# Third quarters of the weights loaded at the first copy, another set of six pairs and a planner that counts SyncE's queue, in a two-layer encoder kernel

## The chip, the cores and the metric

The kernel runs on one core of a Trainium2 chip. The metric is the device time of one execution, in microseconds (us). Three runs of the kernel before have a median of 2688.19 us (2686.57 to 2691.58).

## The reference, cut to what matters

A trunk of two layers works on x, 256 tokens by 4096 channels, in float32. Each layer multiplies the normalised x by one large matrix `w_in` (4096 x 11264), does attention with 16 heads (4 for keys and values) on a part of the result and a bidirectional retention with 8 heads on another, gates both, and multiplies the 4096 channels of the outcome by `w_out` (4096 x 4096). The result is added to x, and a last norm follows.

```python
for l in range(DEPTH):                      # 2 layers
    h = rmsnorm(x, norm_w[l])
    proj = h @ w_in[l]                      # 256 x 4096 by 4096 x 11264
    aq, ak, av, ag, rq, rk, rv, rg = jnp.split(proj, SPLIT_POINTS, axis=-1)
    aq = axial_rope(rmsnorm(aq)) * attn_scale
    ak = axial_rope(rmsnorm(ak))
    a_out = silu(ag) * gqa_attention(aq, ak, av)          # softmax(q k^T) v
    rq, rk = axial_rope(rq), axial_rope(rk) * ret_scale
    r = bidirectional_retention(rq, rk, rv, log_gf, log_gb)
    r_out = silu(rg) * rmsnorm(r, ret_norm[l])
    x = x + jnp.concatenate([a_out, r_out], axis=-1) @ w_out[l]
return rmsnorm(x, final_norm)
```

## The kernel before, in words

**The products.** The columns of the two weight matrices are cut into blocks of 1024 (two times 512): 11 blocks of `w_in` and 4 of `w_out` in each layer, 30 in all. A block runs over 16 pairs of row tiles (a pair is 256 rows of weights), and adds up in eight banks, `M1` to `M8`. A float32 weight is not multiplied as it is: ScalarE casts it to a rounded high half (`whi`), VectorE subtracts that from the weight to make the low half (`wlo`), and each product is three matmuls, high by high (weights `whi`, operand `x8h` or `x7h`), high by low (`x8l` or `x7l`) at L1605, and low by high at L1615.

**Eights and sevens.** Ten of the 16 pairs of a block, the eights, have eight products and two pages of weights; a page is 128 x 1024 numbers (512 KB) and is loaded by SyncE into the tile `wraw` (L490; six places). The other six pairs, the sevens (the table `SEVENS`, L91), use a scheme with seven products in place of eight. They need sums of the weights' quarters: page A is the first load (`wraw`; two quarters), page T the tile `wv`, made by ScalarE as a copy of A (L643), to which GpSimd (POOL) adds the second quarter by an accumulating DMA (L645, issued by `add` at L663). The *third quarter* is loaded by SyncE into the tile `third` (256 KB, L507; two places). Page U (`wu`) is A plus `wv` plus `third`, two additions on VectorE (L601 and L602). Page B is the third quarter itself, of which `bhi` (ScalarE) and `blo` (VectorE) are the halves, one place each (L553). There are 30 x 6 = 180 third quarters.

**The order.** Every engine takes its instructions in the order in which the program is written, and this order is set by a planner in the program itself. It keeps an estimated time `now.t` for TensorE, and for VectorE (`ve`) and ScalarE (`ac`) an estimated time until which they are busy (`Clock`, L273). Constants stand for what loads take: `RAW_LANDING` (6.0 us) for a `wraw` or `third`, `ADD_LANDING` (11.0 us) from the end of the copy `wv` to the accumulated sum.
- `load` (L484) issues the next `wraw` as soon as the low half of an old one is written (`empty`). 
- `begin` (L582) makes the halves of a page. With page A of a seven it raises `wanted` and calls `load_third` (L501), which issues the load of the third quarter if one of the two places is free; a place counts as free when the matmuls on page B are done (`release`, L517, which raises `done`). With page T it writes the two additions of `wu` and has VectorE's estimate wait for `wv` and `third` (L600).
- `halve` (L620) makes the halves of page B once the page before has been released and `wu` has been written.
- `add_up` (L630) makes the copy `wv` when A has landed by the estimate, up to two ahead (`SUMS`).
- `low_parts` writes the low halves that are due; `parts` (L550) keeps them in the list `later`, with a function `then` that is called behind the low half.

**The other work.** Attention, retention, norms and stores run as tasks between the products of a block: `tick` (L1001) runs a step when `room` finds time for it. `startable` (L952) names the next task to begin: if the pages of a task don't suffice, a later one may go ahead, except past a task that needs `STRICT` or more pages. `AT_ONCE` (L83) says up to how many tasks `running` (L967) counts when it lets another begin. The sequences of such a task: the attention scores `attention_pair` (L1165) take one free bank of `M1`, `M5`, `M6`, `M7` between two blocks (`take_bank`, L886), multiply into it (L1081 to L1083), VectorE takes the maximum (`st`), ScalarE the exponentials (`pr`), and the bank is free again. `attention_values` (L1210) fetches the turned exponentials (`pT`, L1048), splits them and multiplies them with the values. `combine` frees `M1` at the end of a block by a copy to `ca`. `retention_head` (L1336) takes a bank only if `LONG` more products than usual are left until it is needed.

**The opening.** In the first block of each of the four stages (two layers, `w_in` and `w_out`) the six sevens stand at the places that the tables `SPREAD` to `SPREAD3` name, since the operand x still arrives in chunks.

Most operations of VectorE and ScalarE are recorded at L289, in the helper that keeps the estimates, so they are told apart by their tiles.

Of the kernel before, what the change touches and what calls it, by code (L numbers as in the profile page):

```python
# [39 lines left out]
THIRDS = 2  # L40

RING = 5

STRICT = 9
RELIEF = 2.0
ADDED = 99
AHEAD = 6
# [16 lines left out]
MARGIN = 0.0  # L64

RAW_LANDING = 6.0
ADD_LANDING = 11.0
ADD_SLACK = 0.3

RUSH = 1.0  # L70
# [9 lines left out]
TIGHT_A = 2  # L80
TIGHT_B = 9

AT_ONCE = 3  # L83

WARM = 20

# [1 line left out]

START = 1

SEVENS = ((3, 5, 7, 9, 11, 13), (3, 5, 7, 9, 11, 13), (3, 5, 7, 9, 11, 13), (3, 5, 7, 9, 11, 13))  # L91

EVER = sorted(set(_p for _s in SEVENS for _p in _s))
EIGHTS = [_p for _p in range(NP) if _p not in EVER]
# [11 lines left out]

QUEUE = 1.0
LOW_AHEAD = 3.0
LONG = 2

NEAR = 30

# [68 lines left out]
GROUPS = [  # L181
    ([tuple(range(_s[0]))] if _s[0] else []) + [tuple(range(_a, _b)) for _a, _b in zip(_s, _s[1:] + (NP,))] for _s in SEVENS
]
SPREAD = (3, 6, 9, 10, 12, 14)
SPREAD1 = (4, 6, 8, 9, 11, 13)
SPREAD2 = (2, 4, 6, 7, 10, 12)
SPREAD3 = (5, 7, 8, 11, 12, 14)


# [114 lines left out]
def hybrid_encoder(  # L304
# [141 lines left out]
    class Weights:  # L446


        def __init__(self):
            self.pages, self.sevens = [], []  # L450
            for l in range(DEPTH):
                for w, n in ((w_in, N_IN), (w_out, N_OUT2)):
                    for b in range(n):
                        stage = 2 * l + (w is w_out)
                        start = (l, b) == (0, 0) and w is w_in
                        for g in GROUPS[stage] if b else FIRST_GROUPS[stage]:
                            for slot in slots_of(g, stage, start):
                                one = Page()
                                one.pair, one.kind, one.uses, one.left = slot[0][1], slot[0][3], len(slot), 3 * len(slot)
                                one.whole = start and one.pair in NATIVE  # L460
                                one.seven = one.pair in SEVENS[stage] and not one.whole
                                one.begun, one.low_at, one.empty = False, None, False
                                one.kept, one.half, one.own = None, one.seven and one.kind == PAGE_B, None
                                if w is w_out and (l, b) == (DEPTH - 1, n - 1) and one.pair in DELAYED:
                                    one.kept = 0 if one.kind == PAGE_A else 1
                                    one.uses, one.left = one.uses - 1, one.left - 3
                                if one.seven:
                                    if one.kind == PAGE_A:
                                        self.sevens.append(Seven(w[l, b, one.pair]))
                                    one.own = self.sevens[-1]  # L470
                                if not one.seven or one.kind == PAGE_A:
                                    one.src = w[l, b, one.pair, int(one.kind == PAGE_B)]
                                self.pages.append(one)
            self.wholes = [g for g in self.pages if g.whole]
            self.thirds = [g for g in self.pages if g.half]
            self.seq = [g for g in self.pages if not g.whole and not g.half]
            self.raws = [g for g in self.seq if not g.seven or g.kind == PAGE_A]
            self.placed, self.emptied, self.made = 0, 0, 0
            self.credit, self.at, self.granted, self.summed = 0, 0, 0, 0
            self.loaded, self.halved, self.done, self.wanted = 0, 0, 0, 0  # L480
            self.lows, self.spent = 0, 0
            self.later, self.adds = [], []

        def load(self):  # L484

            if self.placed < len(self.raws):
                g = self.raws[self.placed]
                self.placed += 1
                g.raw = t(wp, [P, 2, NB], "wraw", RAWS)
                nc.sync.dma_start(g.raw, g.src)  # L490
                if g.seven:
                    g.own.a, g.own.a_at = g.raw, max(now.t, ve.until) + RAW_LANDING

        def empty(self, g):

# [4 lines left out]

        def load_third(self):  # L501

            while self.loaded < min(self.wanted, self.done + THIRDS):
                o = self.thirds[self.loaded].own
                self.loaded += 1
                o.b = t(wp, [P, NB], "third", THIRDS)
                nc.sync.dma_start(o.b, o.third)  # L507
                o.b_at = now.t + RAW_LANDING

        def grant(self):  # L510

# [5 lines left out]
        def release(self, g):  # L517

            if g.half:
                self.done += 1  # L520
                self.load_third()
                self.halve()
                return
            self.credit += 1
# [57 lines left out]
        def begin(self, g):  # L582

            g.begun = True
            if not g.seven:
                self.parts(g, g.raw, then=partial(self.empty, g))
                return
            o = g.own
            if g.kind == PAGE_A:
                self.wanted += 1  # L590
                self.load_third()
                ac.after(o.a_at)
                self.parts(g, o.a)
# [14 lines left out]
            else:  # L608
                ac.after(o.u_at)
                self.parts(g, o.u)  # L610

        def spend(self):
            self.spent += 1

# [5 lines left out]
        def halve(self):  # L620

            if self.halved == self.done < len(self.thirds):
                g = self.thirds[self.halved]
                if g.own.u_at:
                    self.halved += 1
                    g.begun = True
                    ac.after(g.own.b_at)
                    self.parts(g, g.own.b)

        def add_up(self, until=None):  # L630

            while self.summed < len(self.sevens):
# [5 lines left out]
                elif not o.a or o.a_at > now.t or ac.until > now.t + 4.0 or self.summed >= self.spent + SUMS:  # L638
                    return
                self.summed += 1  # L640
                o.v = t(wp, [P, 2, NB], "wv", SUMS)
                ac.after(o.a_at)
                ac.copy(o.v, o.a)  # L643
# [1360 lines left out]
```

## Time and profile before

| | us |
|---|---|
| median of three runs | 2688.19 |
| lowest, highest | 2686.57, 2691.58 |
| profiled execution, its own time | 2683.35 |
| its span, first to last instruction | 2681.6 |

| engine | busy us | instructions |
|---|---|---|
| PE (TensorE matmuls) | 2613.6 | 11560 |
| PEld (TensorE weight loads, beside PE) | 2136.4 | 11560 |
| DVE (VectorE) | 2197.0 | 2702 |
| ACT (ScalarE) | 1847.1 | 2634 |
| POOL (GpSimd) | 457.8 | 548 |

The mean granted clock of TensorE is 0.994 of full speed. The DMA engines carried 657.72 MB. Where a row reads `DVE wu L289 <- DMA third<-in_w_in: 116.2, 57, 6.6`, VectorE waited before the instructions that write `wu` for the load of `third` from the matrix `w_in`: 116.2 us in total, 57 times, 6.6 us at the longest. In a row of the timeline stand the start and the length of an instruction, and in square brackets the idle time of its engine ahead of it and what ended that. In a row of the windows stand the stretch, its length, the busy time of PE, PEld, DVE, ACT and POOL (with the instructions that began there), the granted clock, the share of the DMA engines and GB/s.

### The profile page before, as it was taken

The page shows a single profiled execution, that of the slowest core. Times are in us where ns is not written, and L with a number is a line of the kernel's source. Part 1 is how long each engine was busy: PE and PEld are TensorE (multiplying, and loading weights), DVE is VectorE, ACT ScalarE, POOL GpSimd, SP SyncE. Part 2 cuts the span into 40 slices and gives each one's busy share as a digit, 9 for nine tenths or more (in the row PEclk, how much of TensorE's full clock was granted, in tenths as well). Part 3 has the DMA queues.
Part 4 walks back from the last instruction along what each step waited for, and adds up shares of the span by engine and source line. Part 5 has one row for each costly group of instructions (what it writes and reads, how often), then busy time and mean ns, then how long its engine had stood idle before and what let it go on. Part 6 is the DMA issues. An engine that isn't in the chain of part 4 may idle for free.

```text
span 2681.6 us, 34374 instructions
## 1 busy us (share of the span) xinstructions
PE 2613.6 (97%) x11560; PEld 2136.4 (80%) x11560; DVE 2197.0 (82%) x2702; ACT 1847.1 (69%) x2634; POOL 457.8 (17%) x548
## 2 busy tenths in 40 slices
PE   9999999999999999999999999999999999999997
PEld 6788877787888888788778888877788888888875
DVE  6898888888878898777978888878887888987767
ACT  7876776666666788656876667766676668776654
POOL 0111321221112101211111212311211121010110
PEclk9999999999999999999999999999999999999999
DMA  8988978888688867888888878888976787778885
GB/s 292 284 244 271 281 233 267 273 242 251 208 237 238 248 210 219 260 260 246 271 245 230 261 238 285 248 256 251 280 232 209 216 269 227 216 213 257 230 247 166
DMA packets 229634, 657.72 MB, mean 245 GB/s; under 512 B 24784, under 2 KB 31440, under 8 KB 229456
## 3 DMA queue, kind: packets, MB, share of 16 engines
q1 hardware_dynamic: 147040, 472.99, 50.2%
q0 software_dynamic: 81696, 181.44, 30.5%
q8 instruction: 90, 1.47, 0.2%
q10 hardware_dynamic: 720, 1.10, 0.1%
q14 instruction: 88, 0.72, 0.1%
HBM read 611.39 MB, written 44.04 MB: 244 GB/s over the span
## 4 chain that ended last, share of the span: by engine, by line
PE 38%; DMA 5%; DVE 4%; issue 2%; ACT 1%; SPq 0%; POOL 0%; DVEq 0%; POOLq 0%; ACTq 0%
PE M L1605 24%; PE M L1615 12%; DVE wlo L289 3%; DMA third<-in_w_out 2%; DMA third<-in_w_in 2%; DMA wv<-in_w_in 1%; PE M L1081 1%; ACT whi L289 0%; PE M L1083 0%; PE M L1082 0%; DVE cb L289 0%; ACT ca L289 0%; DVE ca L289 0%; DVE rot L289 0%; DVE wu L289 0%
## 5 line engine op out<-in xcount | busy, mean ns | idle before, releaser
L289 DVE TENSOR_TENSOR wlo<-wraw,whi 128x1024 fp32r<-128x1024 f32 (+1 forms) x776 | 934.2, 1212 | 124.6 <-PE M L1615 64.8
L289 ACT CAST whi<-wraw 128x1024 fp32r<-128x1024 f32 (+1 forms) x776 | 797.3, 1044 | 236.9 <-PE M L1605 216.2
L1605 PE MATMUL M<-whi,x8h 128*128 128x512 f32 x2368 | 926.7, 391 | 3.3 <-DVE cb L289 2.8
L1605 PE MATMUL M<-whi,x8l 128*128 128x512 f32 x2368 | 924.6, 390 | 0.0
L1615 PE MATMUL M<-wlo,x8h 128*128 128x512 f32 x2368 | 681.0, 391 | 5.9 <-DVE wlo L289 5.8
L1605 PEld LDWEIGHTS M<-whi,x8h 128*128 128x128 f32 x2368 | 446.4, 189 | 102.2 <-ACT whi L289 5.6
L1615 PEld LDWEIGHTS M<-wlo,x8h 128*128 128x128 f32 x2368 | 443.4, 188 | 100.7 <-DVE wlo L289 10.1
L1605 PEld LDWEIGHTS M<-whi,x8l 128*128 128x128 f32 x2368 | 446.2, 188 | 93.0 <-issue 0.2
L1605 PE MATMUL M<-whi,x7h 128*128 128x512 f32 x1080 | 423.3, 392 | 11.0 <-ACT whi L289 6.5
L1605 PE MATMUL M<-whi,x7l 128*128 128x512 f32 x1080 | 422.2, 391 | 0.0
L663 POOL DMA_DIRECT2D wv<-in_w_in x132 | 162.6, 1232 | 1269.8 <-ACT wv L289 1009.2
L1615 PE MATMUL M<-wlo,x7h 128*128 128x512 f32 x1080 | 339.0, 395 | 17.8 <-DVE wlo L289 17.1
L289 DVE TENSOR_TENSOR wu<-wu,third 128x512 f32<-128x512 f32 x180 | 124.6, 692 | 187.2 <-DMA third<-in_w_in 116.2
L1615 PEld LDWEIGHTS M<-wlo,x7h 128*128 128x128 f32 x1080 | 200.8, 189 | 73.0 <-DVE wlo L289 33.4
L289 ACT CAST bhi<-third 128x512 fp32r<-128x512 f32 x180 | 111.6, 620 | 211.3 <-DMA third<-in_w_in 139.4
L1605 PEld LDWEIGHTS M<-whi,x7h 128*128 128x128 f32 x1080 | 203.6, 188 | 57.3 <-ACT whi L289 11.1
L1605 PEld LDWEIGHTS M<-whi,x7l 128*128 128x128 f32 x1080 | 203.8, 189 | 42.1
L289 ACT CAST whi<-wv 128x1024 fp32r<-128x1024 f32 x180 | 188.5, 1047 | 66.4 <-DMA wv<-in_w_in 27.4
L289 DVE TENSOR_TENSOR wlo<-wu,whi 128x1024 fp32r<-128x1024 f32 x180 | 219.1, 1217 | 14.7 <-ACT whi L289 8.8
L289 DVE TENSOR_TENSOR wlo<-wv,whi 128x1024 fp32r<-128x1024 f32 x180 | 219.0, 1217 | 14.6 <-ACT whi L289 7.6
L289 ACT CAST whi<-wu 128x1024 fp32r<-128x1024 f32 x180 | 188.9, 1050 | 47.9 <-DVE wu L289 27.8
L289 ACT COPY wv<-wraw 128x1024 f32<-128x1024 f32 x180 | 188.6, 1048 | 43.9 <-DMA wraw<-in_w_in 19.7
(238 smaller groups left out, 2342.7 us busy)
## 6 DMA issues: line engine op xcount, KB each, us to landing
wraw<-in_w_in SPq DMA_DIRECT2D x568, 512.0 KB, 4.9
wraw<-in_w_out SPq DMA_DIRECT2D x208, 512.0 KB, 4.8
wv<-in_w_in POOLq DMA_DIRECT2D x132, 512.0 KB, 7.8
third<-in_w_in SPq DMA_DIRECT2D x132, 256.0 KB, 5.6
wv<-in_w_out POOLq DMA_DIRECT2D x48, 512.0 KB, 8.2
third<-in_w_out SPq DMA_DIRECT2D x48, 256.0 KB, 5.8
full<-next_dram POOLq DMA_DIRECT2D x18, 512.0 KB, 9.6
kv<-kv_dram POOLq DMA_DIRECT2D x16, 512.0 KB, 10.0
```

The source lines that it names most:

```text
L289: return call(out, *args, **kwargs)
L663: self.adds.pop(0)[1]()
L1081: nc.tensor.matmul(out, a[0], b[0], start=start, stop=False)
L1605: nc.tensor.matmul(acc[name], a[i], g.hi[h], start=m == first[name] and not i, stop=False)
L1615: nc.tensor.matmul(acc[name], a, g.lo[h], start=False, stop=m == final[name])
```

## The change

- `add_up` calls `load_third` when it writes the copy `wv`, one to two sevens ahead of page A's own step, and `begin` no longer raises `wanted` by itself beyond that.
- A place of `third` counts as free when `blo` has been written (`third_split`, called as `then` of page B), not when page B's matmuls have been written.
- `issued` keeps an estimate `queue` of SyncE's issues, 0.35 us (`ISSUE`) each, for both kinds of load. A page of an eight has ScalarE's estimate wait for its load (`ac.after(g.raw_at)`).
- `ADD_LANDING` goes from 11.0 to 9.5, `STRICT` from 9 to 4, `AT_ONCE` from 3 to 2, `LONG` from 2 to 4.
- The sevens are pairs 2, 5, 8, 9, 11, 12 in place of 3, 5, 7, 9, 11, 13, and three of the four `SPREAD` tables change.

The products, the halves and the loads are of the same kinds and numbers as before.

```diff
-STRICT = 9
+STRICT = 4
-ADD_LANDING = 11.0
+ISSUE = 0.35
+ADD_LANDING = 9.5
-AT_ONCE = 3
+AT_ONCE = 2
-SEVENS = ((3, 5, 7, 9, 11, 13), ...)
+SEVENS = ((2, 5, 8, 9, 11, 12), ...)
-LONG = 2
+LONG = 4
-SPREAD = (3, 6, 9, 10, 12, 14)
+SPREAD = (4, 5, 9, 10, 12, 14)
...
@@ load
                 nc.sync.dma_start(g.raw, g.src)
+                g.raw_at = self.issued(ve.until)
                 if g.seven:
-                    g.own.a, g.own.a_at = g.raw, max(now.t, ve.until) + RAW_LANDING
+                    g.own.a, g.own.a_at = g.raw, g.raw_at
+        def issued(self, free):
+            self.queue = max(self.queue, now.t, free) + ISSUE
+            return self.queue + RAW_LANDING
@@ load_third
-            while self.loaded < min(self.wanted, self.done + THIRDS):
+            while self.loaded < min(self.wanted, self.split_thirds + THIRDS):
...
-                o.b_at = now.t + RAW_LANDING
+                o.b_at = self.issued(0.0)
@@ release
                 self.done += 1
-                self.load_third()
@@ begin
             if not g.seven:
+                ac.after(g.raw_at)
...
             if g.kind == PAGE_A:
-                self.wanted += 1
+                self.wanted = max(self.wanted, self.sevens.index(o) + 1)
+        def third_split(self):
+            self.split_thirds += 1
+            self.load_third()
@@ halve
-                    self.parts(g, g.own.b)
+                    self.parts(g, g.own.b, then=self.third_split)
@@ add_up
                 self.summed += 1
+                self.wanted = max(self.wanted, self.summed)
+                self.load_third()
                 o.v = t(wp, [P, 2, NB], "wv", SUMS)
```

The change moves instructions on every engine. Numbers behind a tile's name run in the order in which the program is written; L289 and L490 of before are L290 and L491 now, L507 is L514.

SyncE, in a block of `w_in` in the second layer: from the load of the first quarter of the block's fourth seven (the first row) to the load of its third quarter (the last). `wraw` is a page, `third` a third quarter. Before:

```order
L490 DMA wraw_16669<-in_w_in 128x1024
L490 DMA wraw_16679<-in_w_in 128x1024
L490 DMA wraw_16711<-in_w_in 128x1024
L507 DMA third_16726<-in_w_in 128x512
L490 DMA wraw_16764<-in_w_in 128x1024
L490 DMA wraw_16774<-in_w_in 128x1024
L490 DMA wraw_16807<-in_w_in 128x1024
L507 DMA third_16816<-in_w_in 128x512
```

and SyncE in the same block now:

```order
L491 DMA wraw_16566<-in_w_in 128x1024
L491 DMA wraw_16575<-in_w_in 128x1024
L491 DMA wraw_16606<-in_w_in 128x1024
L491 DMA wraw_16632<-in_w_in 128x1024
L491 DMA wraw_16646<-in_w_in 128x1024
L514 DMA third_16656<-in_w_in 128x512
```

The third quarter stood seven rows behind its first quarter, with another third quarter between, and stands five rows behind it now.

ScalarE, at the scores of an attention group of the first layer (`ca` is the copy that frees bank `M1`, `pr` the exponentials of a score bank, `M1` with a number the score in that bank). Before, one of the groups:

```order
L289 COPY ca_3937<-M1_3454 128x512
L289 CAST whi_3940<-wu_3899 128x1024
L289 ACTIVATE pr_3932,st_3931<-M1_3955,st_3931,rs_3475 128x256 x2
L289 CAST whi_3969<-wraw_3815 128x1024
L289 CAST whi_3992<-wraw_3837 128x1024
L289 ACTIVATE pr_3932,st_3931<-M1_3984,st_3931,rs_3475 128x256 x2
```

and ScalarE at the last group of the same layer now (`pTh` is the high half of the fetched `pT`):

```order
L290 CAST pTh_5392<-pT_5283 128x1024
L290 CAST whi_5402<-wraw_5239 128x1024
L290 COPY ca_5413<-M1_4934 128x512
L290 CAST whi_5416<-wu_5373 128x1024
L290 ACTIVATE pr_5000,st_4999<-M1_5431,st_4999,rs_4180 128x256 x2
L290 CAST whi_5445<-wraw_5267 128x1024
L290 ACTIVATE pr_5000<-pr_5000,st_4999 128x256 x4
L290 ACTIVATE pr_5451,st_5450<-M1_5465,st_5450,rs_4180 128x256 x2
L290 CAST whi_5485<-wraw_5312 128x1024
L290 CAST whi_5497<-wraw_5376 128x1024
L290 ACTIVATE pr_5451,st_5450<-M1_5509,st_5450,rs_4180 128x256 x2
```

Two scores followed each other on the bank `M1` there, three do here, and the cast of `pT` stands ahead of `ca`.

VectorE, in a block of the first layer, from one `blo` to the next. Before:

```order
L289 TENSOR_TENSOR blo_3648<-third_3581,bhi_3647 128x512
L289 TENSOR_TENSOR wlo_3673<-wu_3617,whi_3656 128x1024
L289 TENSOR_TENSOR wlo_3689<-wraw_3520,whi_3671 128x1024
L289 TENSOR_TENSOR wu_3697<-wraw_3520,wv_3593 128x512
L289 TENSOR_TENSOR wu_3697<-wu_3697,third_3669 128x512
L289 TENSOR_TENSOR wlo_3706<-wraw_3526,whi_3687 128x1024
L289 TENSOR_TENSOR wlo_3725<-wv_3593,whi_3702 128x1024
L289 TENSOR_TENSOR wlo_3741<-wraw_3571,whi_3723 128x1024
L289 TENSOR_TENSOR blo_3731<-third_3669,bhi_3730 128x512
```

and VectorE in the first layer now, between two sevens that are neighbours:

```order
L290 TENSOR_TENSOR blo_3728<-third_3605,bhi_3727 128x512
L290 TENSOR_TENSOR wlo_3754<-wu_3701,whi_3737 128x1024
L290 TENSOR_TENSOR wlo_3768<-wraw_3583,whi_3752 128x1024
L290 TENSOR_TENSOR wu_3770<-wraw_3583,wv_3669 128x512
L290 TENSOR_TENSOR wu_3770<-wu_3770,third_3667 128x512
L290 TENSOR_TENSOR wlo_3785<-wv_3669,whi_3775 128x1024
L290 TENSOR_TENSOR wlo_3801<-wu_3770,whi_3783 128x1024
L290 TENSOR_TENSOR wlo_3817<-wraw_3592,whi_3799 128x1024
L290 TENSOR_TENSOR blo_3807<-third_3667,bhi_3806 128x512
```

Between the two `blo` stood two pages of the eight that lies between the sevens (both from `wraw`); now pages of sevens alone stand between, one more of them a `wu`.

More of the change, by code (lines that the diff above doesn't have):

```diff
@@ L183 @@
 ]
-SPREAD = (3, 6, 9, 10, 12, 14)
-SPREAD1 = (4, 6, 8, 9, 11, 13)
-SPREAD2 = (2, 4, 6, 7, 10, 12)
+SPREAD = (4, 5, 9, 10, 12, 14)
+SPREAD1 = (7, 8, 10, 11, 13, 14)
+SPREAD2 = (2, 3, 6, 9, 10, 12)
 SPREAD3 = (5, 7, 8, 11, 12, 14)
@@ L480, in __init__ @@
             self.loaded, self.halved, self.done, self.wanted = 0, 0, 0, 0
-            self.lows, self.spent = 0, 0
+            self.lows, self.spent, self.split_thirds, self.queue = 0, 0, 0, 0.0
             self.later, self.adds = [], []
```

2 lines of the change are left out of this document (1 added, 1 removed).

## The prediction

> **What bounds the kernel now.** I read the page first, then the list of waits, then what waits for the tile `third`, and at last the timeline of single stalls. The page:
>
> ```profile
> span 2681.6 us, 34374 instructions
> PE 2613.6 (97%) x11560; PEld 2136.4 (80%) x11560; DVE 2197.0 (82%) x2702; ACT 1847.1 (69%) x2634; POOL 457.8 (17%) x548
> PE 38%; DMA 5%; DVE 4%; issue 2%; ACT 1%; SPq 0%; POOL 0%; DVEq 0%; POOLq 0%; ACTq 0%
> ```
>
> TensorE is the bound, and the change takes no matmul away, so all that can be won is the time in which it waits. The chain names a transfer (5%) and VectorE (4%) as what holds it up. The list of waits says which:
>
> ```profile
> ACT bhi L289 <- DMA third<-in_w_in: 139.4, 50, 7.9
> DVE wu L289 <- DMA third<-in_w_in: 116.2, 57, 6.6
> DVE wu L289 <- DMA third<-in_w_out: 67.2, 25, 8.4
> PEld M L1615 <- DVE wlo L289: 43.5, 49, 3.8
> ACT bhi L289 <- DMA third<-in_w_out: 41.6, 14, 8.1
> DVE wlo L289 <- ACT whi L289: 33.2, 30, 3.3
> PE M L1615 <- DVE wlo L289: 23.0, 30, 3.3
> ```
>
> VectorE sits 183.4 us (116.2 + 67.2) before the sum `wu` until a third quarter has landed, ScalarE 181.0 us before `bhi`. Both engines take their work in order, so the low halves `wlo` behind the sum come late, and TensorE waits for those. One such place, the worst: the issue of the quarter and its landing (chain of waits), VectorE behind it, the matmul behind that (timeline), and the clock around this and one other stall (windows; the column before the last two is the granted clock):
>
> ```profile
> 1928.99 10.71 DMA third<-in_w_in
> ```
>
> ```profile
> 1939.79 0.69 DVE L289 TENSOR_TENSOR wu<-wu,third 128x512 f32<-128x512 f32 x1 [6.60 <-DMA third<-in_w_in]
> 1940.40 1.22 DVE L289 TENSOR_TENSOR wlo<-wv,whi 128x1024 fp32r<-128x1024 f32 x1
> ```
>
> ```profile
> 1937.71 0.39 PE L1605 MATMUL M<-whi,x7h 128*128 128x512 f32 x1
> 1937.94 0.39 PE L1605 MATMUL M<-whi,x7l 128*128 128x512 f32 x1
> 1941.67 0.80 PE L1615 MATMUL M<-wlo,x7h 128*128 128x512 f32 x1 [3.34 <-DVE wlo L289]
> ```
>
> ```profile
> 1107.00:1111.00 4.00, 1.71 (x9) 1.09 (x8) 2.23 (x3) 1.77 (x3) 0.61 (x1) 1.00 1.05 362
> 1111.00:1115.00 4.00, 4.00 (x12) 3.15 (x11) 4.00 (x5) 3.32 (x4) 0.77 (x1) 0.58 1.04 277
> 1937.00:1941.00 4.00, 1.33 (x6) 0.75 (x4) 1.21 (x2) 1.02 (x2) 0.00 (x0) 1.00 1.02 324
> 1941.00:1948.00 7.00, 6.33 (x15) 4.99 (x16) 6.90 (x7) 5.66 (x9) 0.00 (x0) 0.51 1.00 310
> ```
>
> The quarter was on its way for 10.71 us while the DMA engines were full (share 1.02). Two matmuls that follow each other without a wait start 0.23 us apart (1937.71 and 1937.94 here), so this wait cost 1941.67 - 1937.94 - 0.23 = 3.5 us, and then the clock stood at 0.51 for 7 us, which loses 7 x 0.49 = 3.4 us more. After the stall at 1107 to 1111 it is 4 x 0.42 = 1.7 us.
>
> **The change: the third quarters.** SyncE's rows, shown with the change, have the quarter of the fourth pair seven rows behind the load of its first quarter before, five now. Over all 180 quarters seven rows is the commonest distance before (118 of them) and three or four now (111). In matmuls between the load's place in the program and that of the sum that reads it, the median goes from 20 to 49, at 0.23 us each from 4.5 to 11 us (an estimate from the order and that spacing). What a load of `third` needs from its issue to its landing:
>
> ```profile
> DMA to landing us min/median/max: 3.4/5.7/15.3
> ```
>
> 4.5 us is less than the median landing, 11 us nearly twice it; 15 of the 180 now keep less than 8 us. So nearly all waits on `third` should go. Their price to TensorE: the waits for `wlo` cost it at least the 23.0 us that PE idles, at most the 43.5 us that the weight loads idle. A load runs one matmul ahead, so I take 43.5 - 49 x 0.23 = 32 us. Of VectorE's waits that feed it (183.4 for the quarter, 33.2 for `whi`, 17.2 for the accumulated `wv`, row below) the quarter has 78%: 25 us. The clock adds 1.7 + 3.4 = 5.1, and 15 of 180 left over give back 2.5. That makes -27.5 us (bounds -15 and -43).
>
> In these two places PE idled 2.3 and 3.34 us and the clock fell after both. [...]
>
> The load waits on SyncE for VectorE's `blo` of two pairs earlier, where it waited for a matmul's release before. Behind it stand `wraw` loads, which wait for later VectorE work anyway, so that wait costs nothing.
>
> **The sum's timing.** The planner now counts 9.5 us, not 11, from the copy `wv` to the accumulated second quarter, and so starts the step that reads it up to 1.5 us earlier.
>
> ```profile
> ACT whi L289 <- DMA wv<-in_w_in: 27.4, 17, 4.7
> ACT whi L289 <- DMA wv<-in_w_out: 18.5, 9, 4.0
>   DVE wu L289: 17.2, 7
> ```
>
> 26 waits on ScalarE (45.9 us) and 7 on VectorE, which may each grow by 1.5 us: 50 us of engine waits. The 364 us of waits on `third` cost TensorE about 30, or 0.08 of their length: +4 at that rate. Nothing if the copies also run earlier. I take +2.5 (bounds 0 and +8).
>
> **The scores.** With two tasks at once and a strict queue from four pages on, the attention scores of a group are placed differently (ScalarE's rows, shown with the change). In the group of the rows of now three scores follow each other on one bank, 12 to 16 matmuls (2.7 to 3.6 us) apart, where a group had one such pair before: 22 successions in all now, 8 before. The next score must wait for the exponentials of the one ahead of it. A place of before:
>
> ```profile
> PEld M L1081 <- ACT pr L289: 10.7, 6, 2.6
> ```
>
> ```profile
> 443.52 0.68 DVE L289 TENSOR_REDUCE st<-M 128x2 f32<-128x512 f32 x1
> 445.05 0.55 ACT L289 ACTIVATE pr<-M,st,rs 128x256 f32<-128x256 f32 x1
> ```
>
> From the maximum to the second exponential's end is 445.60 - 443.52 = 2.1 us, so the 2.7 to 3.6 us between suffice unless VectorE has over 0.6 us of other work ahead of the maximum; before, 6 of the 8 did wait, 1.8 us each (10.7 over 6), mostly just behind a late quarter. If all 22 waited 1.8 us, the cost would be 40 - 10.7 = +29; if VectorE is now on time, 0. I take +6.
>
> In the rows of now the cast of `pT` stands ahead of `ca`, which frees the bank for the score. Its fetch stands 15 matmuls ahead of it in the program, 22 before at the nearest such place, where the trace has fetch and cast 13.4 us apart:
>
> ```profile
> 602.54 0.56 POOL L1048 DMA_DIRECT2D pT<-p_dram  x1
> 615.97 1.04 ACT L289 CAST pTh<-pT 128x1024 fp32r<-128x1024 f32 x1
> ```
>
> And from its issue to its landing `pT` takes
>
> ```profile
> DMA to landing us min/median/max: 6.7/11.8/16.7
> ```
>
> 7 matmuls less leave 11.8 us, just the median landing. The place comes once a layer: 0 to 8 us each, I take 2, so +4.
>
> **The other six pairs.** Pairs 8, 9 and 11, 12 are now neighbours. `bhi` and `blo` have one place, so those of the second can only be made when the matmul of the first has read them. In VectorE's rows, shown with the change, five `wlo`, the two halves of `wu` and a `blo` stand from one `blo` to the next. By the durations of the page and of the timeline above (1.22, 0.69) and with `blo` taken like a half of `wu`, that is 5 x 1.22 + 3 x 0.69 = 8.2 us of work, and TensorE has only 21 matmuls (4.8 us) from the one `blo` to the next; before, an eight stood between (45 matmuls, 10.2 us). VectorE must be some 3 us ahead here, which it mostly is if no quarter stops it. `blo` stands 9 matmuls or fewer ahead of its use at 35 places now, 6 before.
>
> ```profile
> PEld M L1615 <- DVE blo L289: 1.9, 2, 1.4
> ```
>
> Between nothing and 29 more places x 0.95 (1.9 over 2) = +28; I take +3, since the total work is unchanged. The opening (other SPREADs) has one stall before, 29 to 34 us (windows), with ScalarE's wait for a transfer ahead of it (timeline):
>
> ```profile
> 27.84 1.05 ACT L289 COPY wv<-wraw 128x1024 f32<-128x1024 f32 x1 [5.47 <-DMA wraw<-in_w_in]
> ```
>
> ```profile
> 29.00:34.00 5.00, 1.19 (x5) 0.69 (x5) 3.36 (x8) 4.13 (x9) 1.21 (x1) 0.90 0.93 236
> 34.00:41.00 7.00, 7.00 (x20) 5.39 (x20) 6.96 (x12) 6.97 (x12) 0.00 (x0) 0.58 0.63 209
> ```
>
> PE is busy for 1.19 of 5 us, then the clock loses 7 x 0.42 = 2.9: -6.7 if all of it goes. The copy waits for the transfers, which the new order makes no smaller, and it asks for one chunk of x earlier: 0, between -6.7 and another such idle time, +3.8.
>
> **The sum.** -27.5 + 2.5 + 6 + 4 + 3 = -12 us on the profiled execution (2683.35 us, of which the span is 2681.6), so 2671. The three runs have a median of 2688.19 (2686.57 to 2691.58), 4.8 above the profiled one; against it, 2676 us.
>
> **Rivals.** (1) The waits on `third` were also what put VectorE behind at the scores, so that nothing is lost there: -27.5 + 2.5 = -25, 2663 us. For it: the score stalls of before stand behind late quarters. Against: the new rows leave less between scores.
> (2) The transfers trade places: the engines are full near the sums (share 1.02 at 1937), and a quarter of 256 KB put ahead holds the loads behind it up by 256 KB / 324 GB/s = 0.8 us each. 180 x 0.8 = 145 us of later `wraw` and `wv`, at 0.08 +12 us: 2688 us, no change. [...] Against: the mean rate is 245 GB/s, so there is room between:
>
> ```profile
> DMA packets 229634, 657.72 MB, mean 245 GB/s; under 512 B 24784, under 2 KB 31440, under 8 KB 229456
> ```
>
> (3) Slower: the one bank. If VectorE has over 0.6 us of low halves ahead of the maximum at each of the 22 successions, they cost the full +29, and with it `pT` comes 4 us late in each layer (+8): -27.5 + 29 + 8 + 3 + 2.5 = +15, 2703 us. It decides from where the sum passes 5.4 us: 22 x 1.4 - 10.7 = 20, so from 1.4 us a succession on.
> That the quarters don't move earlier is excluded by the rows.
>
> **The numbers.** Forecast 0.42, rival 1 0.20, rival 2 0.20, rival 3 0.18. Faster by over 0.2% (5.4 us, about what a measurement of this kernel can tell from no change): 0.62; within: 0.20; slower: 0.18. The range from 2656 to 2695 holds the forecast, rivals 1 and 2 and the weak end of rival 3; left out are the strong end of rival 1 with a good opening (0.06) and the rest of rival 3 (0.12).
>
> **What would show it.** In the profile after: `wu` and `bhi` wait under 40 us in all for `third` (364 before); PEld's wait for `wlo` falls below 20; the clock row keeps 1.00 through the middle. If the waits on `third` go and PEld's wait for `wlo` stays, the term of 25 us was wrong. PEld's wait at the scores (L1081 before) tells the forecast (some 17 us) from rival 1 (10 or less) and rival 3 (over 30); longer landings of `wraw` and waits on `wv` would be rival 2.

## The result and the profile after

| | before | changed |
|---|---|---|
| median of four runs, us | 2689.89 | 2670.82 |
| lowest, highest | 2686.57, 2694.27 | 2665.83, 2676.23 |
| profiled execution | 2683.35 | 2665.83 |
| its span | 2681.6 | 2664.1 |

The ratio is 0.9929, with a 95% interval from 0.9903 to 0.9954: 19 us faster, 17.5 us between the two profiled spans. The prediction was 12 us faster (2676 us, range 2656 to 2695). Each profile is one execution, and the four runs of the changed kernel alone lie 10 us apart, so terms of a few us read from two profiles hold for these two executions only. The page after:

```profile
span 2664.1 us, 34300 instructions
PE 2606.1 (98%) x11560; PEld 2136.2 (80%) x11560; DVE 2222.3 (83%) x2702; ACT 1839.3 (69%) x2621; POOL 458.1 (17%) x548
PE 12%; DVE 1%; issue 1%; ACT 1%; POOL 0%; POOLq 0%; DVEq 0%; ACTq 0%
```

TensorE is busy for 7.5 us less (its matmuls overlap: in the prediction's rows they start 0.23 us apart and last 0.39 us; the one at 1941.67, where the granted clock was 0.51, lasted 0.80) and idle for 10 us less. The chain can be followed back over only some 15% of the span now; no transfer, 5% before, is in that part. The tile `third` (idle time of the engines ahead of its readers, then issue to landing) says why:

```profile
  DMA third<-in_w_in: 10.4, 7
DMA to landing us min/median/max: 2.6/6.6/11.8
```

10.4 us of waits where 364 stood. The quarter does not land faster (a median of 6.6 us, 5.7 before); it is asked for earlier. What TensorE's weight loads now wait for:

```profile
PEld M L1094 <- ACT ca L290: 14.9, 4, 7.0
PEld M L1628 <- DVE wlo L290: 14.4, 23, 2.1
PEld M L1094 <- ACT pr L290: 14.0, 16, 1.7
PEld M L1628 <- DVE blo L290: 9.6, 8, 1.8
PEld M L1618 <- ACT bhi L290: 6.4, 7, 1.2
PEld M L1618 <- ACT whi L290: 2.1, 3, 1.0
```

and those rows of before that the prediction did not show:

```profile
PEld M L1605 <- ACT whi L289: 16.7, 15, 4.2
PEld M L1081 <- ACT ca L289: 5.3, 4, 2.3
PEld M L1605 <- ACT bhi L289: 3.2, 3, 1.2
```

With 0.23 us taken off each wait, as in the prediction (in both traces the median weight load starts 0.22 us ahead of its own matmul, and each behind the start of the matmul before), TensorE's account is:

| what is waited for | before, us | after, us | difference | forecast |
|---|---|---|---|---|
| `wlo` | 32.2 | 9.1 | -23.1 | -22.4 |
| `whi` | 13.2 | 1.4 | -11.8 | with the opening, 0; with the sum's timing, +2.5 |
| `pr`, the scores | 9.3 | 10.3 | +1.0 | +6 |
| `ca`, behind `pT` | 4.4 | 14.0 | +9.6 | +4 |
| `blo` and `bhi` | 3.9 | 12.6 | +8.7 | +3 |

The sum is -15.6. The clock adds some -2: the mean, 0.9943 to four digits, loses 15.3 us of 2681.6, and 0.9949 loses 13.5 of 2664.1. Together that is -17.4 against the measured -17.5. The rows of a few us that the table leaves out would add some +2, so the account is no closer than that.

The two largest new stalls stand where the prediction put them, at the late `pT`. This is the one in the first layer. ScalarE waits for the fetch, then casts it, and only then frees the bank by `ca` (timeline, ScalarE, then TensorE):

```profile
606.36 1.04 ACT L290 CAST pTh<-pT 128x1024 fp32r<-128x1024 f32 x1 [5.36 <-DMA pT<-p_dram]
607.31 1.04 ACT L290 CAST whi<-wraw 128x1024 fp32r<-128x1024 f32 x1
608.25 0.58 ACT L290 COPY ca<-M 128x512 f32<-128x512 f32 x1
```

```profile
604.23 0.39 PE L1628 MATMUL M<-wlo,x8h 128*128 128x512 f32 x1
608.88 0.38 PE L1094 MATMUL M<-kv,aqh 128*128 128x256 f32 x1 [4.27 <-ACT ca L290]
```

The one in the second layer is 6.59 us, at 1925.67. The opening's stall is gone (windows as in the prediction):

```profile
29.00:34.00 5.00, 5.00 (x24) 4.14 (x23) 4.45 (x8) 4.89 (x8) 0.00 (x0) 1.00 1.07 297
34.00:41.00 7.00, 7.00 (x31) 5.41 (x30) 6.34 (x8) 6.97 (x11) 0.00 (x0) 1.00 0.77 291
```

PE is busy for all of the 5 us of which 1.19 were busy before, and the clock stays at 1.00.

### The profile page after: what moved, and what is told of

Read it like the earlier page. It is cut to its first block, busy times and chain, and to the rows that moved or that the text cites. A ratio compares the mean times of both kernels' runs of the same rounds, so it can differ in the third digit from the quotient of the medians.

```text
span 2664.1 us, 34300 instructions
## 1 busy us (share of the span) xinstructions
PE 2606.1 (98%) x11560; PEld 2136.2 (80%) x11560; DVE 2222.3 (83%) x2702; ACT 1839.3 (69%) x2621; POOL 458.1 (17%) x548
## 5 line engine op out<-in xcount | busy, mean ns | idle before, releaser
L290 DVE TENSOR_TENSOR wlo<-wraw,whi 128x1024 fp32r<-128x1024 f32 (+1 forms) x776 | 936.1, 1214 | 152.7 <-PE M L1628 62.5
L290 ACT CAST whi<-wraw 128x1024 fp32r<-128x1024 f32 (+1 forms) x776 | 797.0, 1044 | 248.0 <-PE M L1618 199.4
L290 ACT CAST whi<-wv 128x1024 fp32r<-128x1024 f32 x180 | 189.1, 1051 | 140.7 <-DMA wv<-in_w_in 61.8
L290 ACT COPY wv<-wraw 128x1024 f32<-128x1024 f32 x180 | 188.9, 1050 | 120.0 <-DVE wlo L290 59.5
L290 ACT CAST whi<-wu 128x1024 fp32r<-128x1024 f32 x180 | 189.1, 1051 | 112.9 <-DVE wu L290 87.3
L290 DVE TENSOR_TENSOR wlo<-wu,whi 128x1024 fp32r<-128x1024 f32 x180 | 219.8, 1221 | 32.5 <-PE M L1628 17.0
L1618 PEld LDWEIGHTS M<-whi,x7h 128*128 128x128 f32 x1080 | 203.1, 188 | 43.5 <-ACT whi L290 1.4
L290 DVE TENSOR_TENSOR wlo<-wv,whi 128x1024 fp32r<-128x1024 f32 x180 | 219.4, 1219 | 18.9 <-PE M L1628 12.4
L290 DVE TENSOR_TENSOR wu<-wraw,wv 128x512 f32<-128x512 f32 x180 | 123.3, 685 | 36.2 <-DMA wv<-in_w_in 18.4
L290 DVE TENSOR_TENSOR blo<-third,bhi 128x512 fp32r<-128x512 f32 x180 | 123.4, 686 | 13.0 <-ACT bhi L290 13.0
```

The lines of the kernel that those rows point to most:

```text
L290: return call(out, *args, **kwargs)
L1618: nc.tensor.matmul(acc[name], a[i], g.hi[h], start=m == first[name] and not i, stop=False)
```

## The experiments

The theory after the result: the quarters' earlier loads earn some 25 us, the `pT` place and the neighbouring pairs give 18 back, and the opening adds 7. The rival: the other set of pairs and the planner's new constants earn the gain, and the quarters only trade places with other loads. Each of the twelve kernels was timed together with the kernel before on one chip, in four batches on three chips, so kernels of different batches are compared by their ratios.

| kernel | ratio to before | 95% interval |
|---|---|---|
| the change | 0.9929 | 0.9903 to 0.9954 |
| before + quarters | 0.9915 | 0.9895 to 0.9935 |
| before + quarters + new tables | 0.9916 | 0.9901 to 0.9931 |
| before + quarters + new tables + new pairs | 0.9934 | 0.9913 to 0.9956 |
| the change without the estimate of SyncE's queue | 0.9914 | 0.9896 to 0.9933 |
| the change, three tasks at once | 0.9921 | 0.9908 to 0.9935 |
| the change, 18 us for fetches | 0.9931 | 0.9911 to 0.9950 |
| before + quarters + estimate | 1.0057 | 1.0040 to 1.0074 |
| the change, old pairs and tables | 1.0023 | 1.0009 to 1.0037 |
| ... and old task constants | 1.0025 | 1.0014 to 1.0035 |
| ... and ADD_LANDING 11, new task constants | 1.0037 | 1.0024 to 1.0051 |
| the change, old tables | 0.9982 | 0.9971 to 0.9992 |
| the change without the quarters | 1.0490 | 1.0463 to 1.0516 |

**The quarters alone.** The kernel before with this part of the diff and nothing else:

```diff
-            while self.loaded < min(self.wanted, self.done + THIRDS):
+            while self.loaded < min(self.wanted, self.split_thirds + THIRDS):
...
-                    self.parts(g, g.own.b)
+                    self.parts(g, g.own.b, then=self.third_split)
...
                 self.summed += 1
+                self.wanted = max(self.wanted, self.summed)
+                self.load_third()
```

> The kernel before with the third quarters' part of the change alone: loaded at the copy, places free at the low half; the set of pairs, the tables, the constants and SyncE's estimate are as before. Theory (the quarters earn it, the rest of the change gives some back): waits on third fall from 364 us to under 40, TensorE's stalls behind late low halves from about 36 us to about 11, and the stall of the opening stays; before less 25 us, a ratio of 0.991 to before (0.988 to 0.994), so as fast as the whole change or faster. Rival (the other set of pairs and the planner's new constants earn it, and the quarters only trade places with other loads): ratio 1.000 (0.998 to 1.002), the low halves late as before, behind waits on wv or wraw.

Measured: 0.9915, so the rival falls; this part alone is as fast as the whole change. What TensorE waits for (weight loads):

```profile
PEld M L1610 <- ACT whi L289: 26.7, 22, 4.2
PEld M L1620 <- DVE wlo L289: 17.2, 23, 3.0
PEld M L1086 <- ACT ca L289: 12.9, 7, 3.6
PEld M L1086 <- ACT pr L289: 3.6, 4, 1.1
```

`wlo` falls by 20 us (32.2 to 17.2 - 23 x 0.23 = 11.9) and `pr` by 6.6 (to 2.7): the late quarters had stood behind the scores too, as the first rival of the prediction had it. `whi` rises by 8.4 (to 21.6) and `ca` by 6.9 (to 11.3). The new wait is that for the accumulated second quarter, and it comes without any change of `ADD_LANDING`. The tile `wv` with the quarters alone, by who waited for it:

```profile
  ACT whi L289: 99.1, 42
  DVE wu L289: 62.1, 32
```

It was 45.9 and 17.2 us before. With the third quarter on time, the second one lands last.

**All of it but the quarters.** The same lines taken back in the changed kernel.

> The changed kernel with the loading of the third quarters as it was before (asked for at page A, place free at the release); all else as changed. Theory: the 25 us come back, waits on third are over 300 us again, TensorE waits over 30 us for low halves; 2671 + 25, ratio 1.002 to before (0.998 to 1.006). Rival (set and constants earn it): ratio 0.993 (0.990 to 0.996).

Measured: 1.0490, 4.9% slower than before. Rival (0.993) and theory (1.002) both miss by far: the quarters are worth 0.85% to the kernel before, but all else of the change without them costs 5%. The waits on `third` (idle ahead of its readers), the mean clock, and the weight loads:

```profile
  DMA third<-in_w_in: 316.5, 101
  DMA third<-in_w_out: 159.8, 48
```

```profile
core 0: 2819.0 us, clock 0.973
```

```profile
PEld M L1627 <- DVE wlo L290: 78.0, 58, 5.4
PEld M L1617 <- ACT x8h L290: 44.8, 10, 9.3
```

Against before, the clock costs 60 us (2819.0 x 0.027 = 76 against 16), `wlo` 32.5 (64.7 against 32.2), and `x8h` 42.5, a wait that before did not have. These three make 135 us, against 137 us between the spans; other rows rose too (`blo` by 15 us, `bhi` by 10) and others fell (`whi` and `pr`), so the match is no closer than some 20 us. `x8h` is the operand of the next product, made by tasks. In the order of the program the first product of a retention pair with its values stands 3510 matmuls from the start, 3126 in the change and 2759 in the kernel before. That the planner put the tasks off since it counts VectorE as waiting for a late quarter is argued from the code; no run tests it alone.

**The old pairs and tables.**

```diff
-SEVENS = ((2, 5, 8, 9, 11, 12), ...)
+SEVENS = ((3, 5, 7, 9, 11, 13), ...)
-SPREAD = (4, 5, 9, 10, 12, 14)
+SPREAD = (3, 6, 9, 10, 12, 14)
...
```

> The changed kernel with the old set of six pairs and the old tables for the opening blocks. Theory: TensorE's stalls for blo and bhi (some 12 us, against 4 before) go back, -8 us; the opening's stall and its lower clock come back, +7 us; the fetch of pT stands 21 matmuls ahead of its cast in place of 15, which takes 1.4 us off each of two stalls, -3; sum -4, 2667, ratio 0.9915 to before (0.989 to 0.994). Rival (the other set earns the gain): ratio 0.998 to 1.002.

The second kernel of this kind takes back the tables alone.

> The changed kernel with the old tables for the opening blocks, the new set of pairs kept. Theory: the stall of the opening (4 us) and the lower clock behind it (2.9 us) come back, and nothing else; +7 us, ratio 0.9955 to before (0.993 to 0.998). Rival (the tables are without effect, the opening went faster by the set of pairs): 0.993.

Measured: 1.0023 and 0.9982. Both are slower than expected; neither the pairs nor the tables are small beside the estimate. The tables are worth 14 us (0.9982 to 0.9929) and not where I had looked: the first block issues its last load 3.4 us later with the old ones (at 87.9 us, 84.5 in the change); the rest is lost in the opening blocks of the later stages. Two of them, with the old tables and with the change (windows):

```profile
980.00:1070.00 90.00, 84.93 (x371) 69.27 (x370) 74.32 (x104) 70.37 (x111) 9.49 (x8) 0.96 0.70 198
1320.00:1410.00 90.00, 84.79 (x351) 66.90 (x352) 73.31 (x100) 73.33 (x121) 11.54 (x11) 0.96 0.79 227
```

```profile
980.00:1070.00 90.00, 89.04 (x403) 73.51 (x402) 76.82 (x103) 71.88 (x115) 9.60 (x8) 1.00 0.75 218
1320.00:1410.00 90.00, 89.05 (x391) 72.82 (x390) 75.45 (x100) 77.04 (x127) 11.59 (x11) 1.00 0.81 237
```

PE is busy for 4 us less in each, and the clock loses 0.04 x 90 = 3.6 us more.

**What costs the old set its gain.** Old pairs with quarters were 0.9915 by themselves and 1.0023 with the new constants and the estimate. Two kernels take back the task constants, and `ADD_LANDING`:

```diff
-STRICT = 4
+STRICT = 9
-AT_ONCE = 2
+AT_ONCE = 3
-LONG = 4
+LONG = 2
```

> The changed kernel with the old set of pairs, the old tables and the old STRICT, AT_ONCE and LONG: what is left of the change are the third quarters, ADD_LANDING 9.5 and the estimate of SyncE's queue. The quarters alone gave a ratio of 0.9915, the old set with all the new constants 1.0023. Theory A (counting 9.5 us to the accumulated sum starts the steps that read it too early: TensorE's stalls of 3.1 to 3.7 us in the blocks of w_out stand behind waits on wv): ratio 1.000 (0.997 to 1.003), waits on wv as in the run with the old set. Theory B (two tasks at once cost it: 4.2 us before the retention's scores in each layer, and more around the tasks): 0.9915 to 0.994.

```diff
-ADD_LANDING = 9.5
+ADD_LANDING = 11.0
```

> The changed kernel with the old set of pairs and the old tables, and ADD_LANDING at 11.0 as before; two tasks at once stay. Theory A: the stalls behind wv in the blocks of w_out (3.1, 3.6, 3.7 and 3.9 us) and the low clock behind them go, -20 to -25 us against the old set with 9.5; ratio 0.993 (0.991 to 0.996). Theory B: 1.002 (0.999 to 1.004).

Measured: 1.0025 and 1.0037. Neither the task constants nor `ADD_LANDING` alone is it: each taken back leaves the loss. So the estimate was put to the test alone, beside the quarters, with every constant as before:

```diff
+ISSUE = 0.35
...
+                g.raw_at = self.issued(ve.until)
...
+        def issued(self, free):
+            self.queue = max(self.queue, now.t, free) + ISSUE
+            return self.queue + RAW_LANDING
...
+                ac.after(g.raw_at)
```

> The kernel before with the third quarters' part and the estimate of SyncE's queue; the set of pairs, the tables and all constants as before (ADD_LANDING 11.0). The quarters alone gave 0.9915; with the estimate and ADD_LANDING 9.5 beside them it was 1.0025. Theory E (the estimate costs it: ScalarE's estimated time runs ahead by the landing of each page, so copies wv come late and TensorE waits behind wv, with the lower clock behind such waits): 1.002 (0.999 to 1.005), 35 us or more at half clock. Theory A (ADD_LANDING 9.5 costs it): 0.9915 (0.989 to 0.994).

Measured: 1.0057, 38 us slower than the quarters alone. The estimate costs it; the mechanism is not the one expected, though. The windows around the turn from the first `w_in` to `w_out`, with the quarters alone:

```profile
860.00:970.00 110.00, 107.42 (x490) 89.08 (x489) 96.33 (x132) 86.23 (x132) 17.00 (x19) 1.00 0.81 243
970.00:1060.00 90.00, 89.11 (x406) 73.25 (x406) 79.59 (x108) 73.35 (x116) 8.63 (x8) 1.00 0.72 212
```

and with the estimate:

```profile
860.00:970.00 110.00, 110.00 (x504) 91.75 (x503) 92.75 (x114) 79.77 (x107) 10.65 (x11) 1.00 0.78 233
970.00:1060.00 90.00, 76.11 (x319) 61.51 (x318) 70.55 (x109) 70.37 (x124) 12.43 (x13) 0.91 0.63 183
```

With the estimate TensorE runs without a gap up to 970 us, and VectorE and ScalarE do less; then PE idles 13.9 us of 90 and the clock falls to 0.91. The order shows what was put off: the products of the second retention pair ahead of the turn stand 3934 matmuls from the start with the quarters alone and 4190 with the estimate. They missed the free banks between two blocks and waited for those after the next block; the operands `x8h` of `w_out` then come late (weight loads, with the estimate):

```profile
PEld M L1618 <- ACT x8h L290: 18.2, 6, 6.5
```

That the same products are put off in the kernel with old pairs and `ADD_LANDING` 11 (4190 there too), and its wait on `x8h` is 17.8 us, fits. In the two kernels with 9.5 they are not (3922), and the loss is elsewhere. A part of it stands in the blocks of `w_out`, where VectorE waits for `wv` and the clock falls behind it: with the old task constants these waits are 25.6 us in all, with the quarters alone 16.0. That they are the whole loss is not shown. One such place, VectorE (timeline) and the windows around it:

```profile
1121.88 0.69 DVE L290 TENSOR_TENSOR wu<-wraw,wv 128x512 f32<-128x512 f32 x1 [6.10 <-DMA wv<-in_w_out]
```

```profile
1122.00:1126.00 4.00, 1.51 (x5) 1.21 (x6) 3.97 (x5) 3.85 (x5) 0.00 (x0) 0.90 0.79 201
1126.00:1130.00 4.00, 4.00 (x14) 3.17 (x13) 4.00 (x5) 3.41 (x4) 1.20 (x1) 0.67 0.82 290
```

Whether 9.5 alone would do this with the old pairs, without the estimate, was not tried and stays open.

**The change without the estimate.**

> The changed kernel without the estimate of SyncE's queue: landings are counted as before, and pages of eights do not push ScalarE's estimate. Set, tables, constants and third quarters as changed. Theory E, in its strong form (the estimate costs 25 us with any set): ratio 0.984 (0.981 to 0.987). Rival (the set and the tables fit the order that the estimate makes, and another order costs them their gain): 0.993 or more, up to 1.000.

Measured: 0.9914, against 0.9929 with it; the intervals overlap. With the new set and tables the estimate costs nothing that can be told, so the strong form of the theory falls: it is a price of the estimate together with the old set and tables. The table of ratios narrows this down: all five programs with early quarters, the estimate and the old tables are at 0.998 or above, the old tables with the new pairs among them, and the three with the estimate and the new tables are at 0.9931 or below. The estimate with the old pairs and the new tables was not tried. The order agrees with the measurement here: in these two programs all products of the retention with its values stand at the same places (the first 3126 matmuls from the start in both), so the estimate puts none of them off.

**Set and tables without the estimate.** The kernel before with the quarters, and the new tables and pairs, or the new tables only:

> The kernel before with the third quarters' part, the new set of pairs and the new tables; no estimate, and all constants as before. Theory (each part's price stands for itself: quarters 0.9915, set and tables -25 us, no estimate): 2642, ratio 0.982 (0.979 to 0.985). Rival (set and tables only give back what the estimate costs, and blo and bhi wait more with neighbouring pairs, +8 us): 0.9915 to 0.995.

> The kernel before with the third quarters' part and the new tables for the opening blocks; the old set of pairs (none of the six are neighbours), no estimate, all constants as before. It differs from the run with the quarters alone (0.9915) by the tables, and from the run with the new pairs too (0.9934) by the set. Theory (neighbouring pairs cost TensorE the waits for blo and bhi, some 13 us there against 3 with the quarters alone; the tables take the opening's stall away, 3 to 7 us): 0.9885 (0.986 to 0.991), blo and bhi together under 5 us. Rival (the time settles near 0.992 whatever the tables and the set, since VectorE's late work only shows in another tile): 0.991 to 0.994, with other stalls in place of those for blo.

Measured: 0.9934 and 0.9916; the rival holds for both. `blo` and `bhi` do as expected, first with the new pairs, then with the tables alone (weight loads):

```profile
PEld M L1610 <- DVE sgT L289: 13.9, 5, 3.6
PEld M L1620 <- DVE blo L289: 9.4, 9, 1.9
PEld M L1610 <- ACT bhi L289: 8.6, 7, 2.3
```

```profile
PEld M L1610 <- ACT bhi L289: 2.3, 2, 1.2
PEld M L1620 <- DVE blo L289: 1.3, 2, 0.7
```

So the neighbouring pairs cause these waits (18.0 us against 3.6). The times differ by 5 us, less than their intervals. The tables help the opening here too (in the first 50 us PE is busy for 45.04 us at a granted clock of 1.00, with the quarters alone for 43.48 at 0.97), and yet the time stays: 0.9916 against 0.9915.

**The late `pT`.** Two kernels fetch it earlier, by the planner's count of a fetch (13 to 18 us), or by three tasks at once:

```diff
-FETCH = 13.0
+FETCH = 18.0
```

> The changed kernel, where the planner counts 18 us in place of 13 from the fetch of pT, q and their like to their use. The fetch of pT stands 59 matmuls or more ahead of its cast, 15 at the least without this edit. Theory (the two stalls of 4.4 and 6.8 us at the scores are the wait of ca behind the cast of a late pT): both go, with them the lower clock behind them (two stretches of 3.4 and 6.8 us, about half of it lost); -11 to -15 us, 2658, ratio 0.988 to before (0.986 to 0.991). Rival (the tasks pushed back by 5 us make others late, and the bank of the scores comes free as late as now): ratio 0.993 with the stall in another place.

```diff
-AT_ONCE = 2
+AT_ONCE = 3
```

> The changed kernel with AT_ONCE at 3 as before; all else as changed. The fetch of pT stands 43 matmuls or more ahead of its cast, 15 at the least in the change. Theory (two tasks at once are what made pT late; a stall of 4.4 and one of 6.8 us and their clock): -11 to -15 us, ratio 0.988 (0.986 to 0.990). Rival (as with the longer count for the fetch, where these stalls went and six others of up to 2.7 us came at the same scores, since the values and the scores of two groups want one bank): 0.993 (0.991 to 0.995).

Measured: 0.9931 and 0.9921 against 0.9929. Both rivals hold. The waits of TensorE (weight loads), first with 18 us for fetches, then with three tasks at once:

```profile
PEld M L1094 <- ACT ca L290: 16.3, 7, 3.1
```

```profile
PEld M L1618 <- DVE sgT L290: 15.9, 6, 2.9
PEld M L1094 <- ACT ca L290: 5.5, 7, 2.4
```

With 18 us the two stalls of up to 7.0 us go and seven of up to 3.1 us take their place; with three at once `ca` falls to 5.5 and a wait of 15.9 us on `sgT` appears, where the values of a group hold the bank. `AT_ONCE` is the constant that made `pT` late, but its late place cost no more than what replaces it.

No kernel here is faster than the change beyond the intervals. The quarters alone give the same gain by the smallest edit.

## Why the prediction was right

**The third quarters, -27.5.** Right in cause, and in size within its bounds. Waits on `third` fell to 10.4 us (under 40 forecast), PEld's on `wlo` to 14.4 (under 20), and the quarters alone gave 0.9915: 22.9 us at a median of 2689.25. The third sign, the clock at 1.00 through the middle, held only in part (0.57 from 609 to 613 us). TensorE's own part in the change is -23.1 against -22.4 (the -27.5 without the 5.1 for the clock). The share of 78% that was given to the quarter was near enough. The 5.1 us for the clock did not stay: the low stretches at 1111 and 1941 us are gone, but the clock gained only 2 us in all, less than the 2.9 of the opening alone, since behind the two stalls at `pT` it was low anew (0.57 from 609 to 613 us, 0.68 from 1926 to 1933).

**The sum's timing, +2.5.** The waits on `wv` did double, from 63 to 129 us on ScalarE and VectorE together (tile `wv` after, by who waited for it):

```profile
  ACT whi L290: 93.1, 48
  DVE wu L290: 36.2, 26
```

They grew even more, to 161 us, with the quarters alone and `ADD_LANDING` at 11. So the reason given, the constant, was wrong; the quarters on time expose them. In the change TensorE does not pay: its wait on `whi` fell.

**The scores, +6.** Too much. PEld's wait there is 14.0 us, between the 17 of the forecast and the 10 of the first rival. 16 of the 22 successions wait, 0.9 us each (14.0 over 16) and not 1.8. That VectorE is on time explains it, which is argued: the gain that the first rival named shows in the quarters alone, where `pr` falls by 6.6 us, and the new placing gives it back. The task constants, to which the prediction put this placing, do not make it. In the order of the programs, the change with old pairs and tables, which keeps the new constants, has 8 such successions, and the quarters with new tables and pairs, which keep the old constants, have 20; so the set of pairs makes them.

**`pT`, +4.** Mechanism and place right, once in each layer, the size too small: +9.6, beside the clock. A median landing was taken for the late case; the fetches of these two places landed 5.4 and 5.8 us after ScalarE was ready.

**The other six pairs, +3.** Mechanism right, size too small: +8.7 for `blo` and `bhi`. The bounds (0 to +28) held it. I left `bhi` out: with one place it waits as `blo` does.

**The opening, 0.** Wrong at its favourable bound: the whole stall went (-6.7), and the tables earn 14 us in all against the old ones in this program, most of it in later opening blocks that the forecast did not look at. The step that failed is that it looked at the first block only, though each of the four stages has a table and three of them change. Beside the quarters alone the same tables earned nothing, so the 14 us are no price of the tables by themselves.

**The sum.** It came out at -12 against -17.5 between the profiles because the errors have both signs: `pT` and the pairs cost 5.6 and 5.7 us more than forecast, the scores 5 less, the opening gained 6.7 that were not counted, the rest of `whi` some 8 more and `wlo` 0.7 more, the 2.5 for the sum's timing were not paid, the 5.1 of the clock did not come and 1.1 more was lost with it. From -12 that leads to -17.4, the account above. That errors of this size cancelled to some 5 us is in part luck. More than that, the sum added the parts as if each had its price. The experiments show that they have not: the estimate of SyncE's queue, which the forecast costed at nothing, costs 38 us with the old set and tables and none with the new; the rest of the change without the quarters costs 5%. The third rival, the one bank, did not happen. The second, transfers that trade places, showed its signs, longer landings and more waits on `wv`, but not its price of 12 us. The landings after (issue to landing, last column):

```profile
wraw<-in_w_in SPq DMA_DIRECT2D x568, 512.0 KB, 5.3
wv<-in_w_in POOLq DMA_DIRECT2D x132, 512.0 KB, 8.8
```

4.9 and 7.8 us before; `wv` lands 1.0 us later, 180 such loads. In the change TensorE's waits show nothing of it; with the quarters alone, where `whi` rose by 8.4 us, they may.

What stays open: why seven quite different programs with early quarters all lie between 0.991 and 0.994 (five more, all with the estimate and the old tables, lie between 0.998 and 1.006). In the runs a wait that was taken away came back in another tile at about the same sum; what sets that sum was not isolated.

## What to carry to other kernels

The late load was charged here to whoever stood behind it in the order of the program: before, VectorE waited 183.4 us for `third` ahead of `wu`, and TensorE's weight loads 43.5 us for the `wlo` behind it; in the change these are 4.3 and 14.4 us. Find such a load by what the late engine waits for, not by what TensorE waits for, and ask for it as far ahead as its place allows. Then look up what lands last once it is on time, here the accumulated copy (waits on `wv` of 63 us before, 129 us after). Where a planner writes the order, a constant has no price of its own: test each part alone and the whole without it, and look in the order for work that just misses a window of free banks: it is then put off by a whole block, and here the estimate that did this cost 38 us.

## What the runs showed of the hardware

The low clock comes in pieces. In the traces of before and after, seven stretches of half clock (granted 0.50) lie behind the first 30 us and ahead of the last 40; four of them last 3.41 us and three 6.83. In the 3.41 us just ahead of each, TensorE had idled between 1.41 and 3.41 us (median 2.7; ends of matmuls are modelled). The stall of 2.3 us from 1107 to 1111 us before had one stretch of 3.41 us behind it, which loses 3.41 x 0.50 = 1.7 us more (an estimate from the two). Not every stall had this: in the kernel with old pairs and `ADD_LANDING` 11 an idle time of 3.21 us had no low clock behind it (timeline, and windows around it):

```profile
1865.97 0.51 PE L1094 MATMUL M<-pTh,kv 128*128 128x512 f32 x1 [3.21 <-ACT ca L290]
```

```profile
1862.50:1866.50 4.00, 0.79 (x4) 0.48 (x3) 3.54 (x5) 3.57 (x5) 0.00 (x0) 1.00 0.44 143
1866.50:1874.00 7.50, 7.50 (x37) 6.09 (x36) 7.50 (x9) 3.43 (x4) 0.00 (x0) 1.00 0.49 152
```

By the clock records of the two traces all stretches, those of the last 40 us too, begin on one grid of 3.413 us in each, to within 0.005 us over up to 774 steps. Cut along that grid from 29 us to the last 40, 1506 parts of both at full clock have full clock in the next part, and in none of them TensorE idled for more than 1.77 us; seven have half clock in the next part, and in none of those it idled for less than 1.41 us. Behind a part at half clock, full clock came back in seven cases, in all of which TensorE had idled for 0.00 us in that part; half clock stayed in three, with 0.62 us or more. So in these two traces the low clock goes with the idle time inside one part, and seven stretches are few to say more. Where on the grid of its own run the idle time of 3.21 us above lay is not shown.
